# U-phase of an expert layer: the high and low parts of the tokens pass the high weights in one 512-column product

## The chip, the cores and the metric

The kernel runs on one core of a Trainium2 chip. The metric is the device time of one execution in microseconds, as a median of several runs. Beside it there is one profiled execution, with a trace of every engine: TensorE (PE, with its weight loads as PEld), VectorE (DVE), ScalarE (ACT), GpSimd (POOL) and SyncE (SP), which issues the loads of the weights.

## The reference, cut to what matters

Two transformer blocks run one after the other on 256 tokens of width 1024. The last part of the second is an expert layer with 16384 experts of one neuron each; it takes about half of the time. The change lies in it alone.

```python
def peer_ffn(h, w_query, sub_keys, expert_u, expert_v):
    q = jnp.einsum('bsd,dk->bsk', h, w_query).reshape(B, S, PEER_HEADS, 2, PEER_HALF)
    sc = jnp.einsum('bshpc,hpnc->bshpn', q, sub_keys, ...)
    s1, i1 = lax.top_k(sc[..., 0, :], PEER_TOPK)          # 16 of 128 keys
    s2, i2 = lax.top_k(sc[..., 1, :], PEER_TOPK)
    ...                                                   # 16 of the 16 x 16 sums
    gates = jax.nn.softmax(top_s, axis=-1)
    def chunk(args):
        u = expert_u[ec]
        a = jax.nn.gelu(jnp.einsum('cd,chkd->chk', xc, u), approximate=False) * wc
        return jnp.einsum('chk,chkd->cd', a, expert_v[ec])
```

## The kernel before

The kernel gathers nothing. It computes the activation of all 16384 experts for all 256 tokens, keeps gelu of it in a tile `G` of 128 x 128 x 256, multiplies `G` by a matrix of gates that is zero for experts not chosen, and multiplies the result by all of `expert_v`.

**Two-part products.** Every float32 operand is split in two parts that TensorE takes at full rate: `split` (L288) makes the high part H by a copy on ACT (L289) and the low part L as the source minus H on DVE (L290). A product is then three matmuls, H by L, H by H and L by H, added up in one PSUM bank (`mm3`, L315).

**The U-phase** (L1683 on) runs over 128 blocks of 128 experts. For block i, `wload` issues one DMA of 512 KB (`raw`), splits it into `wh` and `wl` (three buffers each), and `fm_mm` (L327) multiplies it by the tokens `h = (hH, hL)` in 8 steps of the contraction, with three matmuls of 256 columns each, 24 in all (L323, L324, L325). The bank that takes the result is one of four (`mm`, L1436). ScalarE reads it and applies gelu. For the tokens whose gates are in `G` already (the first `td`), gelu goes to a tile `ge`, and DVE multiplies it into `G` (L1638, L1639); for the others it goes straight to `G` (L1635).

**The background** shares the engines with the U-phase. It is a list `bg`, from which `run(UC)` takes some work after each block, by costs written in the code: first the selection on DVE (`half` and `cand` with their top-16 steps, `rowcol`, `lookup`), then `gates`, which transposes the chosen indices on PE into an `mm` bank of its own (L1584 to L1594), then 64 groups of four tokens (`wgroup`): one-hot matrices on DVE (`onehots`, L1605 to L1608, once for two groups), eight small matmuls on PE (L1619, L1620), and the result times `G`, on DVE for blocks that are done (L1625) and by a copy on ACT for the others (L1627).

**What sets the order.** Each engine works through its own instructions in order. That order is made when the program is built: a scheduler with a timeline of its own mixes the U-blocks and the background, by the order in the code and by what is ready in its timeline. It isn't decided on the chip.

After the U-phase comes the V-phase (L1705 on): 128 blocks with twelve matmuls of 512 columns each (L319 to L321).

Of the kernel before, what the change touches and what calls it, by code (L numbers as in the profile page):

```python
# [6 lines left out]
F32 = mybir.dt.float32  # L7
F32R = mybir.dt.float32r
# [4 lines left out]
AF = mybir.ActivationFunctionType  # L13
# [185 lines left out]
def _build(tc, nc, A, out, stop=99, dbg=None):  # L199
    ctx = ExitStack()  # L200
    mm_, act, dve, pool = nc.tensor.matmul, nc.scalar, nc.vector, nc.gpsimd
# [9 lines left out]
    hB = P("hB", side="right")  # L211
# [6 lines left out]
    hA = big.enter_context(TP("hA"))  # L218
# [27 lines left out]
    def mm_bank(shape=(128, 512)):  # L246
        return bank("mm", shape)
# [49 lines left out]
    def wload(ap, n=1024, p=None, g=None):  # L297
        return wsplit(wraw(ap, n), n, p, g)
# [28 lines left out]
    def fm_mm(ps, w, h, nk=8):  # L327

        for k in range(nk):
            mm3(ps, (w[0][:, k * 128:(k + 1) * 128], w[1][:, k * 128:(k + 1) * 128]),  # L330
                (h[0][:, k], h[1][:, k]), k == 0, k == nk - 1)

    def tm_mm(ps, h, k, c, w, n0, n1, start, stop):

        mm3(ps, (h[0][:, k, c * 128:(c + 1) * 128], h[1][:, k, c * 128:(c + 1) * 128]),
            (w[0][:, n0:n1], w[1][:, n0:n1]), start, stop, False)
# [93 lines left out]
    class Norm:  # L430
# [2 lines left out]


        def __init__(self, hp, gain, shift=None, on_dve=False):
            self.hH = hp.tile([128, 8, 256], F32R, tag="hH", name="hH")
            self.hL = hp.tile([128, 8, 256], F32R, tag="hL", name="hL")
            self.gain, self.shift, self.dve = gain, shift, on_dve
            self.kinds = ("mm",) * 4
            self.h = (self.hH, self.hL)  # L440
            self.s = {}
# [53 lines left out]
    class RawNorm:  # L495
# [3 lines left out]


        def __init__(self, hp, gain):
            self.hH = hp.tile([128, 8, 256], F32R, tag="hH", name="hH")
            self.hL = hp.tile([128, 8, 256], F32R, tag="hL", name="hL")
            self.gain, self.h = gain, (self.hH, self.hL)
            self.ss, self.y, self.v, self.half = {}, {}, {}, {}

# [209 lines left out]
    with TP("warm") as p:  # L716
        z = p.tile([128, 256], BF16, name="z")
        dve.memset(z, 0.0)
        ps = fill_bank((128, 256))
# [62 lines left out]
    def mixer(nin, nout):  # L782
        h = nin.h
# [17 lines left out]
        qrope = m.tile([128, 2, 256], F32, name="qrope")  # L801
        knope = m.tile([128, 4, 256], F32, name="knope")
        vm = m.tile([128, 2, 512], F32, name="vm")
        yH = hA.tile([128, 8, 256], F32R, tag="hH", name="yH")
        yL = hA.tile([128, 8, 256], F32R, tag="hL", name="yL")


        latent = {}
# [393 lines left out]
    def attention(nin, nout):  # L1202
        h = nin.h
# [38 lines left out]
        ps = mm_bank((16, 256))  # L1242
# [103 lines left out]
        pstack.close()  # L1346
        fctx.close()
        set_psum(acc=2, mm=2, sc=2, pt=2)
        yH = hA.tile([128, 8, 256], F32R, tag="hH", name="yH2")
        yL = hA.tile([128, 8, 256], F32R, tag="hL", name="yL2")  # L1350

        def y_tile(dt):

# [105 lines left out]
    def peer():  # L1459
# [168 lines left out]
            state["td"] = t0 + 4  # L1628

        def ublock(i):  # L1630
            ps = mm_bank((128, 256))
            fm_mm(ps, wload(A["pu"][i]), h)
            td = state["td"]
            if td < 256:
                act.activation(G[:, i, td:], ps[:, td:], AF.Gelu)  # L1635
            if td > 0:
                t = ps_.tile([128, 256], F32, tag="ge", name="ge")
                act.activation(t[:, 0:td], ps[:, 0:td], AF.Gelu)  # L1638
                dve.tensor_mul(G[:, i, 0:td], t[:, 0:td], G[:, i, 0:td])  # L1639
            state["cur"] = i + 1  # L1640

        from collections import deque
# [3 lines left out]
        def run(c):  # L1646
            nonlocal credit
            credit = min(credit + c, 4.0)
            while bg and credit > 0:
                cost, f = bg.popleft()  # L1650
                f()
                credit -= cost
# [3 lines left out]
        for i in range(17):  # L1656
            if i < 16:
                query(order[i])
            else:
                ublock(0)  # L1660
            if i == 0:
                continue
            nt = order[i - 1]
            scores()
            done.add(nt)
            for c in range(2):
                bg.append((1.1, lambda nt=nt, c=c: half(nt, c)))
            if nt ^ 1 in done:
                for c in range(2):
                    bg.append((1.4, lambda hd=nt // 2, c=c: cand(hd, c)))  # L1670
            run(QC)
# [9 lines left out]
            if g % 2 and late:  # L1681
                bg.append(late.popleft())
        for i in range(1, 128):  # L1683
            ublock(i)
            run(UC)
        while bg:
            bg.popleft()[1]()
        acc = [[acc_bank() for _ in range(2)] for _ in range(2)]
# [16 lines left out]
        for i in range(128 - VT):  # L1705
            if 8 <= i < 40 and i % 4 == 0:
                mod_step(32 + i // 4 + 6, g2p, g2)
            if i == 64:
                done = finish(G)
            if i == 96:  # L1710

                hs = [hB.tile([128, 2, 1024], F32R, tag=t, name="w" + t) for t in ("hH", "hL")]
                for k in range(2):
                    H, L = (h_[:, k] for h_ in hs)
                    split(wraw(A["pv"][126 + k]), H, L)
                    last.append((H, L))
            a = operands(G[:, i].rearrange("p (c n) -> p c n", c=2))
            w = wload(A["pv"][i], 1024, pv1 if i % 4 == 3 else None)
            for c in range(2):
                for j in range(2):  # L1720
                    out_mm(i, c, j, a[c], w)
# [91 lines left out]
```

## Time and profile before

| | |
|---|---|
| median of 3 runs | 1580.17 us (1578.63 to 1581.3) |
| profiled execution | 1577.72 us |
| its span, first to last instruction | 1575.6 us |
| granted TensorE clock, mean | 0.997 |
| PE busy | 1554.0 us, 99% |
| DVE busy | 1122.9 us, 71% |
| ACT busy | 812.9 us, 52% |
| POOL busy | 91.6 us, 6% |

The time of an execution is 2.1 us longer than the span. Busy shares are averages over the whole program; the stretches differ. In rows of the timeline, an instruction's duration reaches into the next one's, so the room that it takes on its engine is read from start to start.

### The profile page before, as it was taken

How to read it: one execution, taken by the hardware profiler on the slowest of the kernel's cores; microseconds unless marked ns; L12 is line 12 of the kernel's file. 1: busy time of each engine (PE TensorE's matmuls, PEld its weight loads, DVE VectorE, ACT ScalarE, POOL GpSimd, SP SyncE). 2: the span in 40 equal slices, each digit the busy share in tenths (PEclk: the TensorE clock that was granted, in tenths of full speed). 3: DMA queues.
4: the chain of work that ended last, by engine and by line, in shares of the span. 5: the costliest groups of instructions: out<-in, count | busy, mean ns of one | idle time of the engine just before them, and what ended most of it. 6: DMA issues, size and time to landing. Idle time of an engine off the chain costs nothing.

```text
span 1575.6 us, 27238 instructions
## 1 busy us (share of the span) xinstructions
PE 1554.0 (99%) x10352; PEld 1408.1 (89%) x10352; DVE 1122.9 (71%) x2210; ACT 812.9 (52%) x1557; POOL 91.6 (6%) x161
## 2 busy tenths in 40 slices
PE   9999999999999999999999999999999999999998
PEld 7999899879999879997899999999999887888886
DVE  7766768768856656556799989788996566555654
ACT  6444564555445676654554554544445445455543
POOL 1400011100000112011000000000000000000001
PEclk9999999999999999999999999999999999999999
DMA  8777754438976446441455655554456777666762
GB/s 310 251 253 245 254 168 137 141 104 306 336 218 226 157 155 201 134 135 54 179 166 182 185 182 167 161 157 157 156 161 190 256 228 235 193 189 189 221 187 91
DMA packets 84852, 299.94 MB, mean 190 GB/s; under 512 B 9616, under 2 KB 11248, under 8 KB 84336
## 3 DMA queue, kind: packets, MB, share of 16 engines
q1 hardware_dynamic: 81072, 290.92, 57.0%
q10 hardware_dynamic: 3648, 7.28, 1.3%
q8 instruction: 81, 1.33, 0.3%
q14 instruction: 51, 0.42, 0.1%
HBM read 294.95 MB, written 3.15 MB: 189 GB/s over the span
## 4 chain that ended last, share of the span: by engine, by line
PE 89%; DMA 5%; DVE 3%; ACT 2%; issue 1%; POOL 0%; SPq 0%; POOLq 0%; ACTq 0%; DVEq 0%
PE mm L323 15%; PE mm L324 15%; PE mm L325 15%; PE acc L319 12%; PE acc L321 11%; PE acc L320 11%; DMA raw<-in_pv 2%; DMA raw<-in_wmod 2%; ACT wh L289 1%; DVE wl L290 1%; PE acc L1619 1%; PE acc L1620 1%; PE acc L929 1%; PE sc L1271 1%; PE mm L1512 0%
## 5 line engine op out<-in xcount | busy, mean ns | idle before, releaser
L289 ACT ACTIVATE wh<-raw 128x1024 fp32r<-128x1024 f32 (+3 forms) x605 | 528.0, 897 | 539.2 <-PE mm L324 251.7
L290 DVE TENSOR_TENSOR wl<-raw,wh 128x1024 fp32r<-128x1024 f32 (+3 forms) x605 | 610.8, 1026 | 266.0 <-ACT wh L289 262.7
L323 PE MATMUL mm<-hL,wh 128*128 128x256 f32 x1976 | 565.0, 286 | 0.0
L325 PE MATMUL mm<-hH,wl 128*128 128x256 f32 x1976 | 560.0, 284 | 0.0
L324 PE MATMUL mm<-hH,wh 128*128 128x256 f32 x1976 | 559.6, 283 | 0.0
L323 PEld LDWEIGHTS mm<-hL,wh 128*128 128x128 f32 x1976 | 377.5, 191 | 2.8
L324 PEld LDWEIGHTS mm<-hH,wh 128*128 128x128 f32 x1976 | 377.6, 191 | 2.0
L325 PEld LDWEIGHTS mm<-hH,wl 128*128 128x128 f32 x1976 | 377.4, 191 | 0.4
L319 PE MATMUL acc<-wh,aL 128*128 128x512 f32 x648 | 256.1, 395 | 0.7 <-DVE aL L290 0.7
L321 PE MATMUL acc<-wl,aH 128*128 128x512 f32 x648 | 253.6, 393 | 0.0
L320 PE MATMUL acc<-wh,aH 128*128 128x512 f32 x648 | 253.3, 391 | 0.0
L321 PEld LDWEIGHTS acc<-wl,aH 128*128 128x128 f32 x648 | 121.7, 188 | 28.6 <-issue 0.2
L319 PEld LDWEIGHTS acc<-wh,aL 128*128 128x128 f32 x648 | 122.0, 188 | 27.1 <-DVE aL L290 2.5
L320 PEld LDWEIGHTS acc<-wh,aH 128*128 128x128 f32 x648 | 121.7, 188 | 26.7 <-issue 0.5
L319 PE MATMUL acc<-wh,hL 128*128 128x512 f32 x224 | 88.6, 397 | 4.1 <-DVE hL L520 2.3
L320 PE MATMUL acc<-wh,hH 128*128 128x512 f32 x224 | 87.3, 391 | 0.0
L321 PE MATMUL acc<-wl,hH 128*128 128x512 f32 (+1 forms) x224 | 85.2, 390 | 0.0
L290 DVE TENSOR_TENSOR aL<-G,aH 128x256 fp32r<-128x256 f32 x128 | 53.6, 419 | 3.4 <-ACT aH L289 3.4
L319 PEld LDWEIGHTS acc<-wh,hL 128*128 128x128 f32 x224 | 42.1, 188 | 13.5 <-ACT wh L289 2.4
L631 DVE SCALAR_TENSOR_TENSOR macc<-raw,col,macc 128x1024 f32<-128x1024 f32 x28 | 35.9, 1281 | 25.0 <-DMA raw<-in_wmod 24.8
L289 ACT ACTIVATE aH<-G 128x256 fp32r<-128x256 f32 x128 | 51.2, 401 | 4.0 <-PE acc L321 4.0
L594 ACT ACTIVATE sg<-sg 128x256 f32<-128x256 f32 x36 | 14.9, 413 | 69.8 <-DVE sg L593 66.5
(476 smaller groups left out, 1649.7 us busy)
## 6 DMA issues: line engine op xcount, KB each, us to landing
raw<-in_pu SPq DMA_DIRECT2D x128, 512.0 KB, 3.6
raw<-in_pv SPq DMA_DIRECT2D x128, 512.0 KB, 4.3
raw<-in_wmod SPq DMA_DIRECT2D x48, 512.0 KB, 4.9
raw<-in_w1gu SPq DMA_DIRECT2D x36, 512.0 KB, 4.4
raw<-in_w2gu SPq DMA_DIRECT2D x36, 512.0 KB, 4.7
raw<-in_w1d SPq DMA_DIRECT2D x22, 512.0 KB, 4.7
raw<-in_w2d SPq DMA_DIRECT2D x22, 512.0 KB, 4.5
raw<-in_wout SPq DMA_DIRECT2D x16, 512.0 KB, 3.6
```

The costliest lines, as they stand in the source:

```text
L289: act.activation(H, src, AF.Copy)
L290: lasts["low"] = dve.tensor_sub(L, src, H.bitcast(F32))
L319: mm_(ps, aL, bH, start=start, stop=False)
L320: mm_(ps, aH, bH, start=False, stop=False)
L321: lasts["pe"] = mm_(ps, aH, bL, start=False, stop=stop)
L323: mm_(ps, aH, bL, start=start, stop=False)
L324: mm_(ps, aH, bH, start=False, stop=False)
L325: mm_(ps, aL, bH, start=False, stop=stop)
L631: dve.scalar_tensor_tensor(macc[j], raw, K("c", k), macc[j], op0=OP.mult, op1=OP.add)
L929: mm_(ps[:, j, c], k[pr][:, j, sl], q[pr][:, j, sl], start=True, stop=True)
L1271: mm_(ps[:, o:o + n], qa[:, hd, c * 128:c * 128 + 128], ka[:, hd, 0:n], start=True, stop=False)
L1619: mm_(ps[:, j], H[:, j], O[:, j], start=True, stop=False)
```

## The change

The tokens' high and low parts now stand in one tile, `h`, side by side. In each of the 8 steps the high weights pass over both at once, in one matmul of 512 columns into a bank of two halves (high by high in the first, high weights by low tokens in the second). The low weights pass over the high tokens as before, into the first half. The two halves then have to be added: ACT copies the second half to the tile `ge` (now for every block), DVE adds the first half to it, and gelu reads the sum from `ge`. The multiplication of gelu with the gates goes from DVE to GpSimd. This second part, `upart`, stands behind `run(UC)` in the loop, where before the whole block stood ahead of it.

```diff
+    def fm_wide(ps, w, hw, nk=8):
+        for k in range(nk):
+            wH, wL = (w[i][:, k * 128:(k + 1) * 128] for i in range(2))
+            low = lambda: mm_(ps[:, 0], wL, hw[:, 0, k], start=False, stop=False)
+            if k == nk - 1:
+                low()
+            mm_(ps, wH, hw[:, :, k], start=k == 0, stop=k == nk - 1)
+            if k < nk - 1:
+                low()
...
-            self.hH = hp.tile([128, 8, 256], F32R, tag="hH", name="hH")
-            self.hL = hp.tile([128, 8, 256], F32R, tag="hL", name="hL")
+            self.both = hp.tile([128, 2, 8, 256], F32R, tag="h", name="h")
+            self.hH, self.hL = self.both[:, 0], self.both[:, 1]
...
         def ublock(i):
-            ps = mm_bank((128, 256))
-            fm_mm(ps, wload(A["pu"][i]), h)
+            ps = mm_bank((128, 2, 256))
+            fm_wide(ps, wload(A["pu"][i]), n6.both)
+            return ps
+
+        def upart(i, ps):
+            u = ps_.tile([128, 256], F32, tag="ge", name="ge")
+            act.activation(u, ps[:, 1], AF.Copy)
+            dve.tensor_add(u, ps[:, 0], u)
             td = state["td"]
             if td < 256:
-                act.activation(G[:, i, td:], ps[:, td:], AF.Gelu)
+                act.activation(G[:, i, td:], u[:, td:], AF.Gelu)
             if td > 0:
-                t = ps_.tile([128, 256], F32, tag="ge", name="ge")
-                act.activation(t[:, 0:td], ps[:, 0:td], AF.Gelu)
-                dve.tensor_mul(G[:, i, 0:td], t[:, 0:td], G[:, i, 0:td])
+                act.activation(u[:, 0:td], u[:, 0:td], AF.Gelu)
+                pool.tensor_mul(G[:, i, 0:td], u[:, 0:td], G[:, i, 0:td])
             state["cur"] = i + 1
...
-                ublock(0)
+                upart(0, ublock(0))
...
         for i in range(1, 128):
-            ublock(i)
+            ps = ublock(i)
             run(UC)
+            upart(i, ps)
```

The other tiles that share the old tags (`yH`, `yL` and a last pair of weights) are cut from a common tile in the same way. In the order below, L339 and L342 are the matmuls of `fm_wide` (low weights, high weights), L1651 is the new addition, and lines of the background stand 13 higher than before.

On PE, at the end of a U-block behind which a group of the background starts, the order before has three matmuls of 256 columns for each step:

```order
L323 MATMUL mm<-hL,wh 128x256
L324 MATMUL mm<-hH,wh 128x256
L325 MATMUL mm<-hH,wl 128x256
L1619 LDWEIGHTS B
L1619 MATMUL acc<-O,B 128x128
```

and the order now has two for each step, one of 512 and one of 256 columns:

```order
L342 MATMUL mm<-h,wh 128x512
L339 MATMUL mm<-h,wl 128x256 x2
L342 MATMUL mm<-h,wh 128x512
L1632 LDWEIGHTS B
L1632 MATMUL acc<-O,B 128x128
```

The 128 blocks lose 1024 matmuls and their weight loads; the groups of the background are as they were.

On DVE, at the place where the first groups of the background begin (B, BL and O are the one-hot tiles, L1570 to L1573 the lookups), the order before goes from one split of weights (`wl`) to the next after one to four other rows:

```order
L1570 TENSOR_TENSOR G_8535<-G_8535,iob_8551 128x2x256
L290 TENSOR_TENSOR wl_10978<-raw_10975,wh_10977 128x1024
L1607 TENSOR_TENSOR B_10911<-B_10911,slotT_8550 128x1024
L1583 TENSOR_TENSOR G_8535<-G_8535,gs_11970 128x128
L1572 TENSOR_TENSOR G_8535<-G_8535,idxf1_8545 128x2x256
L290 TENSOR_TENSOR wl_11016<-raw_11013,wh_11015 128x1024
L1605 TENSOR_TENSOR B_11048<-ioh_8553,slotT_8550 128x1024
L1608 TENSOR_TENSOR O_11047<-ioh_8553,slotT_8550 128x1024
L1573 TENSOR_REDUCE G_8535<-G_8535 128x32
L1606 TENSOR_TENSOR BL_11049<-B_11048,slotT_8550 128x1024
L290 TENSOR_TENSOR wl_11069<-raw_11066,wh_11068 128x1024
```

and the order now, at the same place, ends with the addition for the U-block whose bank is mm_10737 (L1618 to L1621 are the one-hot matrices, L1638 the product with `G`, L1583 and L1586 lookups):

```order
L1620 TENSOR_TENSOR B_10793<-B_10793,slotT_8542 128x1024
L290 TENSOR_TENSOR wl_10979<-raw_10976,wh_10978 128x1024
L1586 TENSOR_REDUCE G_8527<-G_8527 128x32
L1596 TENSOR_TENSOR G_8527<-G_8527,gs_11595 128x128
L1638 SCALAR_TENSOR_TENSOR G_8527<-acc_10680,G_8527 128x44x4
L1618 TENSOR_TENSOR B_10912<-ioh_8545,slotT_8542 128x1024
L1638 SCALAR_TENSOR_TENSOR G_8527<-acc_10720,G_8527 128x45x4
L1621 TENSOR_TENSOR O_10911<-ioh_8545,slotT_8542 128x1024
L1583 TENSOR_TENSOR G_8527<-G_8527,iob_8543 128x2x256
L1619 TENSOR_TENSOR BL_10913<-B_10912,slotT_8542 128x1024
L1651 TENSOR_TENSOR ge_10763<-mm_10737,ge_10763 128x256
```

The addition before this one, that for the bank mm_10697, stands 33 rows ahead; of the rows between, five are splits of weights, eleven one-hot matrices and seven lookups.

On DVE, late in the U-phase, the order before has the product with `G` of a U-block (L1639) between two splits:

```order
L290 TENSOR_TENSOR wl_13495<-raw_13492,wh_13494 128x1024
L1625 SCALAR_TENSOR_TENSOR G_8535<-acc_13381,G_8535 128x97x4
L1639 TENSOR_TENSOR G_8535<-ge_13371,G_8535 128x168
L1607 TENSOR_TENSOR B_13474<-B_13474,slotT_8550 128x1024
L290 TENSOR_TENSOR wl_13541<-raw_13538,wh_13540 128x1024
```

and the order now has the addition there, for two blocks of the same kind:

```order
L290 TENSOR_TENSOR wl_13531<-raw_13528,wh_13530 128x1024
L1618 TENSOR_TENSOR B_13551<-ioh_8545,slotT_8542 128x1024
L1621 TENSOR_TENSOR O_13550<-ioh_8545,slotT_8542 128x1024
L1651 TENSOR_TENSOR ge_13481<-mm_13440,ge_13481 128x256
L1619 TENSOR_TENSOR BL_13552<-B_13551,slotT_8542 128x1024
L290 TENSOR_TENSOR wl_13578<-raw_13575,wh_13577 128x1024
L1638 SCALAR_TENSOR_TENSOR G_8527<-acc_13470,G_8527 128x111x4
L1620 TENSOR_TENSOR B_13551<-B_13551,slotT_8542 128x1024
L1651 TENSOR_TENSOR ge_13521<-mm_13487,ge_13521 128x256
L1638 SCALAR_TENSOR_TENSOR G_8527<-acc_13510,G_8527 128x112x4
```

The product of gelu and gates is gone from DVE and stands alone on GpSimd, which had nothing to do in the U-phase.

## Rows read from the trace of the kernel before

**Rows 1.** The page: engine, busy us (share of the span) and instructions.

```profile
PE 1554.0 (99%) x10352; PEld 1408.1 (89%) x10352; DVE 1122.9 (71%) x2210; ACT 812.9 (52%) x1557; POOL 91.6 (6%) x161
```

**Rows 2.** Stretches of the U-phase: busy us (instructions) by engine, clock, DMA.

```profile
core 0: us, PE busy (x) PEld busy (x) DVE busy (x) ACT busy (x) POOL busy (x), PEclk, DMA share, GB/s
815.00:930.00 115.00, 115.00 (x960) 115.00 (x960) 104.30 (x371) 57.24 (x86) 0.00 (x0) 1.00 0.59 181
...
950.00:1060.00 110.00, 110.00 (x1023) 108.86 (x1022) 90.81 (x161) 55.61 (x131) 0.00 (x0) 1.00 0.53 162
1060.00:1190.00 130.00, 130.00 (x1220) 128.50 (x1219) 115.11 (x184) 60.17 (x154) 0.00 (x0) 1.00 0.50 158
```

**Rows 3.** The same view, ten microseconds before the first background group.

```profile
920.00:930.00 10.00, 10.00 (x85) 10.00 (x85) 5.48 (x11) 5.09 (x8) 0.00 (x0) 1.00 0.55 168
```

**Rows 4.** Timeline of PE, U-phase, first and last of 36: start us, us, instruction.

```profile
864.74 0.28 PE L323 MATMUL mm<-hL,wh 128*128 128x256 f32 x1
...
868.94 0.28 PE L325 MATMUL mm<-hH,wl 128*128 128x256 f32 x1
```

**Rows 5.** Timeline of PE, V-phase, first and last of 28.

```profile
1399.67 0.39 PE L320 MATMUL acc<-wh,aH 128*128 128x512 f32 x1
...
1405.87 0.39 PE L320 MATMUL acc<-wh,aH 128*128 128x512 f32 x1
```

**Rows 6.** Timeline of PE: one background group, and two matmuls behind it.

```profile
1051.86 0.23 PE L1619 MATMUL acc<-O,B 128*128 128x128 f16 x1
...
1052.29 0.36 PE L323 MATMUL mm<-hL,wh 128*128 128x256 f32 x1
1052.49 0.28 PE L324 MATMUL mm<-hH,wh 128*128 128x256 f32 x1
```

**Rows 7.** Groups by form, 800 to 1200 us: count | busy us, mean ns | idle before.

```profile
L290 DVE TENSOR_TENSOR wl<-raw,wh 128x1024 fp32r<-128x1024 f32 x127 | 155.1, 1221 | 46.2 <-ACT wh L289 45.5
L289 ACT ACTIVATE wh<-raw 128x1024 fp32r<-128x1024 f32 x127 | 134.5, 1059 | 191.1 <-PE mm L324 190.1 <-ACT G L1627 0.9
...
L1608 DVE TENSOR_TENSOR O<-ioh,slotT 128x1024 f16<-128x1024 f16 x32 | 21.8, 682 | 0.0
...
L1635 ACT ACTIVATE G<-mm 128x256 f32<-128x256 f32 x45 | 16.6, 369 | 0.0
L1570 DVE TENSOR_TENSOR G<-G,iob 128x512 bf16<-128x512 bf16 x16 | 10.9, 681 | 0.1
L1573 DVE TENSOR_REDUCE G<-G 128x32 f32<-128x512 bf16 x16 | 10.9, 681 | 1.0 <-PE mm L1586 0.8
...
L1572 DVE TENSOR_TENSOR G<-G,idxf 128x512 bf16<-128x512 bf16 x16 | 6.7, 420 | 0.1
```

**Rows 8.** Timeline of DVE: one block during the selection, from split to split.

```profile
840.89 1.20 DVE L290 TENSOR_TENSOR wl<-raw,wh 128x1024 fp32r<-128x1024 f32 x1
842.01 0.29 DVE L1522 MAX8 vals<-G 128x8 f32<-128x128 f32 x1
...
843.66 1.20 DVE L290 TENSOR_TENSOR wl<-raw,wh 128x1024 fp32r<-128x1024 f32 x1
```

**Rows 9.** Timeline of DVE, where GpSimd works beside it.

```profile
708.94 0.42 DVE L1325 TENSOR_TENSOR y<-mm,psc 128x256 f32<-128x256 f32 x1
709.28 0.68 DVE L290 TENSOR_TENSOR wl<-raw,wh 128x512 fp32r<-128x512 f32 x1
709.88 0.71 DVE L1318 TENSOR_TENSOR pd<-pf,pu 128x16 f32<-128x16 f32 x1
```

**Rows 10.** Timeline of POOL, the same two microseconds.

```profile
709.44 1.12 POOL L1326 TENSOR_TENSOR ga<-ga,y 128x256 f32<-128x256 f32 x1 [1.09 <-DVE y L1325]
```

**Rows 11.** The line of a GpSimd product: count, ns min/median/max, starts, forms.

```profile
L1326 POOL TENSOR_TENSOR ga<-ga,y x8: 732/745/1119, 610.7 to 719.9; 128x256 f32<-128x256 f32 x8
```

**Rows 12.** The same for the gelu product on DVE.

```profile
L1639 DVE TENSOR_TENSOR G<-ge,G x83: 156/285/421, 949.7 to 1214.3; 128x256 f32<-128x256 f32 x9, 128x8 f32<-128x8 f32 x2, 128x16 f32<-128x16 f32 x2, 128x24 f32<-128x24 f32 x2
```

**Rows 13.** The same for the product of group and G on DVE.

```profile
L1625 DVE SCALAR_TENSOR_TENSOR G<-acc,G x64: 334/502/646, 946.6 to 1187.9; 128x180 f32<-128x180 f32 x1, 128x184 f32<-128x184 f32 x1, 128x192 f32<-128x192 f32 x1, 128x196 f32<-128x196 f32 x1
```

More of the change, by code (lines that the diff above doesn't have):

```diff
@@ L501, in __init__ @@
         def __init__(self, hp, gain):
-            self.hH = hp.tile([128, 8, 256], F32R, tag="hH", name="hH")
-            self.hL = hp.tile([128, 8, 256], F32R, tag="hL", name="hL")
+            self.both = hp.tile([128, 2, 8, 256], F32R, tag="h", name="h")
+            self.hH, self.hL = self.both[:, 0], self.both[:, 1]
             self.gain, self.h = gain, (self.hH, self.hL)
@@ L803, in mixer @@
         vm = m.tile([128, 2, 512], F32, name="vm")
-        yH = hA.tile([128, 8, 256], F32R, tag="hH", name="yH")
-        yL = hA.tile([128, 8, 256], F32R, tag="hL", name="yL")
+        y_ = hA.tile([128, 2, 8, 256], F32R, tag="h", name="yH")
+        yH, yL = y_[:, 0], y_[:, 1]
         latent = {}
@@ L1348, in attention @@
         set_psum(acc=2, mm=2, sc=2, pt=2)
-        yH = hA.tile([128, 8, 256], F32R, tag="hH", name="yH2")
-        yL = hA.tile([128, 8, 256], F32R, tag="hL", name="yL2")
+        y_ = hA.tile([128, 2, 8, 256], F32R, tag="h", name="yH2")
+        yH, yL = y_[:, 0], y_[:, 1]
         def y_tile(dt):
@@ L1710, in peer @@
             if i == 96:
-                hs = [hB.tile([128, 2, 1024], F32R, tag=t, name="w" + t) for t in ("hH", "hL")]
+                hs_ = hB.tile([128, 2, 2, 1024], F32R, tag="h", name="wh_")
+                hs = [hs_[:, 0], hs_[:, 1]]
                 for k in range(2):
```

## The prediction

> **What bounds the kernel now.** I read the busy shares first, then the U-phase by stretches, then single blocks. The page has PE busy for 99% of the span and DVE for 71% [rows 1]; a gain has to come out of PE, unless another engine takes over. The stretches show where that can happen: in the U-phase PE has no idle time, and DVE is busy for 104.3 of 115 us during the selection, 90.8 of 110 when the background groups begin and 115.1 of 130 late [rows 2]. GpSimd does nothing there. The reader should see that DVE runs at 83 to 91% beside a full PE: a change that takes from PE and gives to DVE has little room. One hole stands out: DVE is busy for only 5.48 of the 10 us just before the first group begins [rows 3]. Selection was finished by then.
>
> The pace of PE is read from start to start: 35 steps from 864.74 to 868.94 us are 0.1200 us for a matmul of 256 columns [rows 4], so 24 of them make a block of 2.88 us. In the V-phase 27 steps take 6.20 us, 0.2296 us for 512 columns [rows 5]. The durations, 0.28 and 0.39, overlap and are not the pace.
>
> **The change part by part: PE.** Three matmuls of 256 columns took 0.3600 us in each of 8 steps. One of 512 and one of 256 take 0.2296 + 0.1200 = 0.3496, so a block goes from 2.880 to 2.797 us, and 128 blocks save 10.6 us. The trace has no place where the two widths alternate. The upper bound is that 256 more columns cost only their own streaming, 0.1067 us at the granted 2.4 GHz (the clock column is 1.00 [rows 2]): 0.2267 for the wide one, 0.0133 saved in a step, 13.6 us in all. The lower bound is nothing saved; a loss would need a wide matmul of over 0.24 us, and 27 in a row took 0.2296. I take 10.6, since the V-phase row has exactly the wide form. The weights of the group matmuls are untouched; a group puts 1052.49 - 1051.86 - 0.12 = 0.51 us between two U-matmuls [rows 6].
>
> The Trainium skill (TensorE: Matmul & The Clock Gate, Back-to-back issue gap) gives 262 cycles for 256 columns and 518 for 512, as an isolated gap. By it a step would save only 6 cycles, 2.5 ns, and the phase 2.6 us. Rows 4 and 5 show 120.0 and 229.6 ns in place of 109 and 216, so here a fixed part goes with each matmul, and that is what the change removes.
>
> **ACT.** A copy of 256 columns out of PSUM is new for each block, 0.37 us by the gelu row of that shape [rows 7]. With the split (1.06), the two gelus and a group's copy ACT needs about 2.2 us of a block of 2.8 or more. I cost it at nothing; it waited 190 us of the stretch for PE [rows 7]. Should that cover go, each block would show 0.37.
>
> **DVE.** An addition of 256 columns with one operand in PSUM takes 0.42 us, and the next instruction starts 0.34 after it [rows 9]; likewise 0.68 for a one-hot row means a room of about 0.60, and 1.22 for a split about 1.12 to 1.14 [rows 7, 8]. So every block gets 0.34 us more on DVE. What goes is the gelu product: 83 of them at a median of 0.285 [rows 12], with a room of about 0.2, and all of them late. The first 46 blocks lose nothing and gain 0.34.
>
> *Selection.* From 815 to 930 us there were 40 blocks with 104.3 us of DVE, 2.61 each [rows 2]. At the new pace 40 blocks last 111.9 us, and the same work with additions is 104.3 + 13.6 = 117.9. About 6 us of selection don't fit and must move behind. The order now shows this: each block there has one split, one addition and some 1.2 us of selection, together 2.66 us by the rooms above, still below 2.797. Nor is the addition late: the split behind it is for a block three further on, about 2 us before PE needs it. So I expect PE at its full new pace here, and the price later.
>
> *Where the groups begin.* There the lookups left over meet the first one-hot matrices. Between the additions for mm_10697 and mm_10737 DVE has five splits (5.7 us at 1.14), eleven one-hot rows (6.6 at 0.60), seven lookups (five at 0.60, two at 0.34: 3.7), two products with G (0.5) and seven small rows (1.3): 17.8 us. With 0.9 from the end of PE's block to the first addition (the copy's 0.37 and a row or two of DVE), some 1.3 of waits for the transposed indices and for a free split buffer, and 0.34 for the second addition it is 20.3. Meanwhile PE may do four blocks, one of them in the bank that the transposes give back (11.2), four groups (2.0) and the transposes (0.2), 13.4 us; then no bank is free until the second addition. PE stands still for about 6.9 us. I take 6.5. If DVE were ahead at that point, 3; if waits add up, 9.
>
> *Late blocks.* Two blocks now have on DVE two splits (2.28), two additions (0.68), four one-hot rows (2.40) and two products with G (late ones up to 0.646 [rows 13], so 1.0): 6.36, or 3.18 each. PE needs 2.797 + 0.95 x 0.51 = 3.28, with 0.95 groups per block counted in the order (before: 3.37). That fits, barely, if nothing else comes to DVE.
>
> **GpSimd.** The product with the gates takes GpSimd 0.73 to 0.75 us at 256 columns when alone [rows 11], less for fewer; it has the time. The question is what it does to DVE. At 709.44 us such a product starts while DVE splits weights; it lasts 1.12 us, 0.4 longer, and the DVE instruction behind the split, of 16 columns only, lasts 0.71 us and ends when GpSimd ends [rows 9, 10]. The two had excluded each other, and DVE lost about 0.55 us. So a product costs DVE between 0 and 0.55 us at full width, in proportion less at lower td. In the late order an addition or a product with G, which read PSUM, often stands behind the split; I assume that every other product hits: 0.1 to 0.25 us per block. DVE then needs about 3.35 against PE's 3.28 in the last 33 blocks with groups: 2.3 us, of which the lead of the splits takes a little. I take 2.0; the bounds are 0 (no collision) and 10 (all collide: 3.18 + 0.4 - 3.28 = 0.3, times 33).
>
> The Trainium skill (SBUF — State Buffer, Who interferes with whom) has this as a rule: a DVE instruction with two SBUF inputs contends with a GpSimd instruction that reads SBUF, and the second waits until the first is done. Rows 9 and 10 agree, 0.71 us for 16 columns. By that rule the new addition is safe, and the splits and one-hot rows are not; it is the case of the second rival.
>
> **Sum.** -10.6 + 6.5 + 2.0 = -2.1 us on a profiled execution of 1577.72 (span 1575.6 and 2.1 around it): 1575.6. The median of the runs is 2.45 higher than the profiled execution, so 1578.1.
>
> **Rivals.**
> *DVE keeps up.* If the built order is looser than my sum, with the transition at 2 us or less and no collisions, PE's saving stays: -8 to -13 us, about 1569. For it: PE never waited before, at 91% of DVE. Against: the hole of 4.5 us [rows 3] and more are spent.
> *GpSimd's products stop DVE.* From the point where td is over about 100 and DVE's room is under 0.1 us per block, every collision lengthens the U-phase. With all of them hitting in the late blocks (+10), 7 at the transition and the saving of 10.6, it is +6; with 2 or 3 us more among the middle blocks, +9: 1586 to 1589. For it: rows 9 and 10, and 4.68 of DVE's 6.36 us for two late blocks have both inputs in SBUF. Against: GpSimd waits too, and often for an instruction followed by one that reads PSUM.
> *The wide matmul saves nearly nothing.* If 256 and 512 columns cost in proportion when they alternate, 2.6 us are saved, the transition still costs 6.5, the late blocks have room for DVE again, and it is +4: 1584. Against it stand rows 4 and 5.
>
> **How the numbers follow.** A change below 0.2%, 3.2 us, can't be told from none. The forecast, -7 to +2 us, has 0.48, of which 0.18 lies below -3.2 and 0.30 within; its own range is 1573 to 1582. DVE keeps up: 0.22, faster. GpSimd stops DVE: 0.22, slower. The wide matmul saves nothing: 0.04, slower. The remaining 0.04 are other ways to no change. So faster 0.40, same 0.34, slower 0.26. Leaving out the lowest tenth (most of the saving kept) and the highest (over +9), the range is 1569 to 1588.
>
> **What the profile will show.** Wide and narrow matmuls in the U-phase should start 0.35 us apart in pairs, and PE should lose 0.08 us per block during the selection. At the first groups PE should have one or two gaps, about 6 us together, the larger ended by the addition on DVE. DVE should be over 95% busy from there to the last group, with splits or one-hot rows of up to 0.5 us more beside GpSimd's products, and these of more than 1 us. I am wrong if PE shows gaps during the selection (additions too late there), if it shows none at the first groups, or if the late blocks are slower than the 3.37 us of before.

## The result and the profile after

The changed kernel takes 1590.26 us in the median of 6 runs (1586.91 to 1593.73), beside 1580.74 us for the kernel before (6 runs of the same comparison). The ratio is 1.0061, with a 95% interval of 1.0044 to 1.0078: slower by 0.6%. The prediction was 1578.1 us and no change, so it was wrong, and the time lies above its range. The profiled execution took 1587.95 us, 10.2 more than that of before.

The page of the changed kernel, part 1 (compare [rows 1]): PE works 3 us less, DVE 35 us more, ACT 49 us more, GpSimd 80 us more.

```profile
PE 1551.0 (98%) x9328; PEld 1350.6 (85%) x9328; DVE 1157.6 (73%) x2255; ACT 861.9 (54%) x1685; POOL 171.2 (11%) x245
```

The stretches of the U-phase in the changed kernel (columns and stretches as in [rows 2], with 950 to 1060 cut in two):

```profile
815.00:930.00 115.00, 115.00 (x665) 100.53 (x664) 110.98 (x421) 70.95 (x128) 0.00 (x0) 1.00 0.52 182
...
950.00:970.00 20.00, 13.85 (x95) 11.65 (x94) 19.38 (x36) 10.32 (x18) 1.40 (x3) 0.95 0.40 143
970.00:1060.00 90.00, 90.00 (x625) 77.64 (x625) 85.23 (x140) 58.03 (x143) 25.82 (x30) 0.99 0.44 153
1060.00:1190.00 130.00, 130.00 (x925) 111.66 (x924) 126.50 (x187) 79.69 (x196) 36.95 (x40) 1.00 0.46 160
```

PE has no idle time in the selection and none in the late stretch, though DVE is now at 97% in both. All of PE's idle time, 6.15 us, lies where the groups begin (950 to 970). The timeline of PE there, with idle time and what ended it in brackets:

```profile
956.36 0.39 PE L342 MATMUL mm<-h,wh 128*128 128x512 f32 x1
956.93 0.47 PE L342 MATMUL mm<-h,wh 128*128 128x512 f32 x1 [0.18 <-DVE slotT L1606]
...
959.55 0.40 PE L342 MATMUL mm<-h,wh 128*128 128x512 f32 x1
962.11 0.23 PE L1632 MATMUL acc<-O,B 128*128 128x128 f16 x1 [2.17 <-DVE B L1620]
...
963.85 0.22 PE L1633 MATMUL acc<-O,BL 128*128 128x128 f16 x1
967.88 0.77 PE L342 MATMUL mm<-h,wh 128*128 128x512 f32 x1 [3.81 <-DVE ge L1651]
968.45 0.41 PE L339 MATMUL mm<-h,wl 128*128 128x256 f32 x1
968.67 0.63 PE L342 MATMUL mm<-h,wh 128*128 128x512 f32 x1
...
971.23 0.46 PE L342 MATMUL mm<-h,wh 128*128 128x512 f32 x1
```

First PE waits for the bank of the transposed indices, which DVE reads (`slotT`), and for a one-hot matrix, then, with all four banks full, for the addition (L1651). That addition and the one before it in DVE's order:

```profile
948.72 0.42 DVE L1651 TENSOR_TENSOR ge<-mm,ge 128x256 f32<-128x256 f32 x1
...
967.41 0.42 DVE L1651 TENSOR_TENSOR ge<-mm,ge 128x256 f32<-128x256 f32 x1
```

They start 18.7 us apart. After the wait for the addition the pairs of matmuls start 0.64 us apart. The windows of PE say why (us, busy, granted clock, DMA):

```profile
968.00:970.00 2.00, 2.00 (x7) 0.50 0.05 12
970.00:972.00 2.00, 2.00 (x10) 0.66 0.00 0
972.00:974.00 2.00, 2.00 (x19) 1.00 0.00 0
```

For 3.35 us the granted clock is at its lower level, 1.2 in place of 2.4 GHz. Five pairs take 3.35 us (967.88 to 971.23) instead of 1.76, so 1.6 us are lost on top of the 6.15. (Read from start to start, less the pace of the matmul ahead, the three waits took 0.34, 2.33 and 3.97 us, 6.6 in all: the idle times in brackets begin only at the end of a duration, which reaches into the next row.)

Away from there a pair takes 0.352 us. In the timeline of PE during the selection, eleven pairs lie between these two starts, 3.87 us:

```profile
889.71 0.40 PE L342 MATMUL mm<-h,wh 128*128 128x512 f32 x1
...
893.58 0.40 PE L342 MATMUL mm<-h,wh 128*128 128x512 f32 x1
```

That is 2.815 us for a block, against 2.880 [rows 4].

To set a U-phase against another I take the time from the last score matmul ahead of it to the first matmul of the V-phase. In the timeline of PE, before:

```profile
813.18 0.60 PE L1512 MATMUL mm<-G,qT 128*128 128x128 f32 x4
...
1211.98 0.39 PE L319 MATMUL acc<-wh,aL 128*128 128x512 f32 x1
```

and after:

```profile
820.61 0.61 PE L1525 MATMUL mm<-G,qT 128*128 128x128 f32 x4
...
1219.55 0.40 PE L319 MATMUL acc<-wh,aL 128*128 128x512 f32 x1
```

The reader should see that the U-phase did not become longer: 398.8 us before, 398.94 after. The traces lie 7.4 us apart already where it begins, and the V-phase (first to last of these matmuls) adds 2.7: 354.33 before, 357.02 after. Ahead of the U-phase the two kernels issue the same instructions in the same order on every engine. So the experiments had to tell these theories apart: the shared tile costs time in all stages (P, and T for the early ones), the wide product costs time that the first trace doesn't show (W, and K for the start), the place of things in DRAM sets when weights land (D), or the rest is chance in when they land (U, C).

### The profile page after: what moved, and what is told of

Its sections match the earlier page's. It is cut to its first block, busy times and chain, and to the rows that moved or that the text cites. A ratio compares the mean times of both kernels' runs of the same rounds, so it can differ in the third digit from the quotient of the medians.

```text
span 1585.8 us, 25510 instructions
## 1 busy us (share of the span) xinstructions
PE 1551.0 (98%) x9328; PEld 1350.6 (85%) x9328; DVE 1157.6 (73%) x2255; ACT 861.9 (54%) x1685; POOL 171.2 (11%) x245
## 4 chain that ended last, share of the span: by engine, by line
PE 75%; DMA 10%; DVE 8%; issue 3%; ACT 2%; POOL 1%; SPq 0%; POOLq 0%; DVEq 0%; ACTq 0%
PE mm L342 15%; PE acc L319 10%; PE acc L321 10%; PE acc L320 10%; PE mm L339 8%; DMA raw<-in_wmod 6%; PE mm L323 5%; PE mm L324 5%; PE mm L325 5%; DVE wl L290 4%; DMA raw<-in_pv 2%; ACT wh L289 1%; PE acc L1632 1%; PE acc L942 1%; PE acc L1633 1%
## 5 line engine op out<-in xcount | busy, mean ns | idle before, releaser
L342 PE MATMUL mm<-h,wh 128*128 128x512 f32 x1024 | 362.1, 401 | 4.0 <-DVE ge L1651 3.8
L323 PE MATMUL mm<-h,wh 128*128 128x256 f32 (+1 forms) x952 | 271.5, 285 | 0.0
L325 PE MATMUL mm<-h,wl 128*128 128x256 f32 (+1 forms) x952 | 270.3, 284 | 0.0
L324 PE MATMUL mm<-h,wh 128*128 128x256 f32 (+1 forms) x952 | 269.8, 283 | 0.0
L339 PE MATMUL mm<-h,wl 128*128 128x256 f32 x1024 | 268.3, 282 | 0.0
L342 PEld LDWEIGHTS mm<-h,wh 128*128 128x128 f32 x1024 | 186.9, 189 | 38.0 <-DVE ge L1651 4.0
L339 PEld LDWEIGHTS mm<-h,wl 128*128 128x128 f32 x1024 | 194.0, 190 | 9.9
L323 PEld LDWEIGHTS mm<-h,wh 128*128 128x128 f32 (+1 forms) x952 | 181.6, 191 | 2.8
L324 PEld LDWEIGHTS mm<-h,wh 128*128 128x128 f32 (+1 forms) x952 | 181.6, 191 | 2.0
L325 PEld LDWEIGHTS mm<-h,wl 128*128 128x128 f32 (+1 forms) x952 | 181.5, 191 | 0.5
L1657 POOL TENSOR_TENSOR G<-ge,G 128x256 f32<-128x256 f32 (+37 forms) x84 | 80.8, 967 | 377.1 <-ACT G L1640 340.4
L319 PE MATMUL acc<-wh,h 128*128 128x512 f32 x224 | 88.8, 398 | 3.0 <-DVE h L506 1.6
L320 PE MATMUL acc<-wh,h 128*128 128x512 f32 x224 | 87.3, 391 | 0.0
```

What stands on the lines that cost most here:

```text
L319: mm_(ps, aL, bH, start=start, stop=False)
L320: mm_(ps, aH, bH, start=False, stop=False)
L323: mm_(ps, aH, bL, start=start, stop=False)
L324: mm_(ps, aH, bH, start=False, stop=False)
L325: mm_(ps, aL, bH, start=False, stop=stop)
L339: low = lambda: mm_(ps[:, 0], wL, hw[:, 0, k], start=False, stop=False)
```

## The experiments

Times are medians beside the kernel before on the same chip; each ratio has its 95% interval. "Start" is the last score, "U" the U-phase as just defined, "V" the V-phase, each from the one trace of that run.

| run | ratio to before | start | U | V |
|---|---|---|---|---|
| e1_tile_only | 0.9999 (0.9989 to 1.0009) | 817.66 | 398.79 | 355.26 |
| e12_tile_only_again | 0.9988 (0.9977 to 1.0000) | 819.43 | 398.80 | 354.35 |
| e11_before_again | 0.9998 (0.9989 to 1.0008) | 812.83 | 398.80 | 357.97 |
| e17_before_other_dram | 0.9988 (0.9974 to 1.0002) | 817.75 | 398.80 | 355.30 |
| e2_no_addition | 1.0013 (1.0000 to 1.0025) | 817.82 | 390.62 | 355.31 |
| e5_no_addition_again | 0.9990 (0.9977 to 1.0004) | 816.76 | 390.63 | 355.55 |
| e13_no_addition_third | 0.9978 (0.9964 to 0.9992) | 819.04 | 390.64 | 356.01 |
| e14_no_addition_two_tiles_early | 0.9983 (0.9971 to 0.9994) | 825.64 | 390.63 | 356.64 |
| e9_wide_late_no_addition | 1.0005 (0.9990 to 1.0019) | 819.27 | 394.67 | 356.08 |
| e10_wide_early_no_addition | 1.0022 (1.0003 to 1.0040) | 827.33 | 394.81 | 355.74 |
| e3_narrow_first | 1.0051 (1.0037 to 1.0066) | 822.08 | 393.61 | 356.21 |
| e18_narrow_first_again | 0.9994 (0.9984 to 1.0005) | 817.13 | 393.61 | 355.81 |
| e16_narrow_first_two_tiles_early | 0.9995 (0.9982 to 1.0008) | 818.53 | 393.60 | 356.61 |
| e19_narrow_first_two_tiles_again | 1.0009 (0.9994 to 1.0024) | 822.71 | 393.61 | 357.50 |
| after | 1.0061 (1.0044 to 1.0078) | 820.61 | 398.94 | 357.02 |
| e6_after_again | 1.0051 (1.0033 to 1.0068) | 821.70 | 398.99 | 357.21 |
| e15_after_two_tiles_early | 1.0036 (1.0019 to 1.0052) | 817.14 | 398.99 | 358.86 |
| e20_after_other_dram | 1.0034 (1.0020 to 1.0049) | 820.08 | 399.89 | 357.25 |
| e4_routing_on_vector | 1.0112 (1.0092 to 1.0133) | 823.31 | 403.40 | 360.41 |

e1 to e4 shared one chip; so did e5, e6, e9 and e10; e11 to e13; e14 to e17; e18 and e19; e20 had its own.

**e1_tile_only, e12_tile_only_again.** The kernel before with the layout alone, in both classes of normalised tokens, the two `y` tiles and the last weights of the V-phase:

```diff
-            self.hH = hp.tile([128, 8, 256], F32R, tag="hH", name="hH")
-            self.hL = hp.tile([128, 8, 256], F32R, tag="hL", name="hL")
+            self.both = hp.tile([128, 2, 8, 256], F32R, tag="h", name="h")
+            self.hH, self.hL = self.both[:, 0], self.both[:, 1]
```

> The kernel before with only the layout changed: high and low part of the tokens in one tile, all products, additions and routing as before. Theory P (the layout costs): the two traces lie 7.4 us apart already where the U-phase starts (after the last score 820.61 against 813.18) and 2.6 us more behind it, though nothing but the tiles differs there, so this kernel is 7 to 10 us slower than before, about 1589. Theory U (the U-phase costs, the rest is chance in when weights land): 1580.7, within 2 us of before.

> The kernel before with the shared tile alone, for a second trace and time. Theory C: last score anywhere from 813 to 822, median within 0.1% of before. Theory K, if the tile were what moves the start: 817 to 818 again as in its first trace. U-phase 398.8 in either.

1579.68 and 1579.52 us, no difference from before. The shared tile costs nothing; theory P falls.

**e2_no_addition, e5_no_addition_again, e13_no_addition_third.** The changed kernel with

```diff
-            u = ps_.tile([128, 256], F32, tag="ge", name="ge")
-            act.activation(u, ps[:, 1], AF.Copy)
-            dve.tensor_add(u, ps[:, 0], u)
+            ps = ps[:, 0]
```

and from there gelu from `ps` and the product with the gates on DVE, as in before.

> After with the wide product, but GELU takes the half of the high tokens' product straight from PSUM and the routing is back on VectorE: it leaves out the sum with the half of the high weights and low tokens. No copy, no addition, no product on GpSimd. Without the addition TensorE does not stall at the first groups (7.8 us in after: 0.18 + 2.17 + 3.81 idle and about 1.65 of halved clock) and keeps 128 x 0.06 = 7.7 us. Theory P: 1590.3 - 7.8 = about 1582 to 1583. Theory U: 1580.7 - 7.7 = 1573.

> The same kernel as e2_no_addition (it leaves out the sum with the half of the high weights and low tokens), for a second trace. In its first trace the U-phase took 390.6 us against 398.8 before (8.2 saved, last score to first product of the V-phase), yet its median was 3.6 us above before's, at a granted clock of 0.994 to 0.996 in the runs of 1581 to 1584 us against 0.998 to 0.999 in those of 1575. Theory C (weights that land late, outside the U-phase, whatever the kernel): U-phase 390 to 391 again, the rest of the span anything between the lowest and highest seen; a median near 1573 to 1580 this time is as likely as 1583. Theory W (the wide product itself costs time that the first trace did not happen to show): again 1581 to 1584, and the trace shows stretches of halved clock or idle TensorE inside or behind the U-phase.

> The wide product without addition (it leaves out the sum with the half of the high weights and low tokens) a third time, beside the two above on one chip. U-phase 390.6 in either. Medians so far 3.6 us above before's and 1.8 below it, where the U-phase alone should give 8.2 below. Theory C: a median anywhere from 1572 to 1583, its mean over the three nearer to 1575 than to 1582. Theory K: again 5 to 10 us later than before outside the U-phase, so 1577 to 1583, last score 816 to 827.

In three traces the U-phase lasts 390.6 us, 8.2 less than before, and PE waits for nothing in it. The stretch where the changed kernel stood still, in e2_no_addition (columns as above):

```profile
950.00:970.00 20.00, 20.00 (x135) 17.23 (x135) 19.87 (x39) 11.08 (x25) 0.00 (x0) 1.00 0.49 166
```

DVE is as full as in the changed kernel, 19.87 of 20 us, but a bank no longer waits for DVE. So the stall comes from the addition, not from PE's pace. The medians, 1582.87, 1578.54 and 1577.12 us, do not show the 8.2 us: 3.6 more than before, then 1.8 and 2.6 less. The expectation of theory C, a mean nearer to 1575 than to 1582, failed: the mean of the three is 1579.5. Theory K's 1577 to 1583 and its start of 816 to 827 held in e13.

**e3_narrow_first, e18_narrow_first_again.** The first some 50 blocks are those of before:

```diff
+            if state["td"] < 16:
+                narrow(i)    # three products of 256 columns, gelu from PSUM
+                run(UC)
+                continue
             ps = ublock(i)
```

> After, but every block before the fifth group (some 50 blocks: the selection and the first groups) goes with the three narrow products of before and GELU straight from PSUM; the wide product, its addition and GpSimd's product only from there on. Takes the stall at the first groups away (7.8 us) and gives 50 x 0.06 = 3 us of the saving back. Theory P: 1590.3 - 7.8 + 3 = about 1585.5. Theory U: 1580.7 - 78 x 0.06 = about 1576. If the stall only moves to the first wide block: 1590 as after.

> The same as e3_narrow_first, beside e19 on one chip. Theory T (the shared tile in the early stages costs): 1586 to 1588 again and 6 to 8 us above e19. Theory C (chance in the start): within 3 us of e19, both 1577 to 1584. U-phase 393.6.

The U-phase is 393.6 us, 5.3 less than after, and PE shows no wait in it: the stall did not move to the first wide block. The time was 1587.24 us in the first run and 1579.32 in the second, on another chip, with the same U-phase. An interval from runs on one chip does not cover this.

**e4_routing_on_vector.**

```diff
-                pool.tensor_mul(G[:, i, 0:td], u[:, 0:td], G[:, i, 0:td])
+                dve.tensor_mul(G[:, i, 0:td], u[:, 0:td], G[:, i, 0:td])
```

> After with the routing product back on VectorE, GpSimd idle. If GpSimd's products hold VectorE up and that decides (the rival of the prediction), this is 3 to 8 us faster than after, 1582 to 1587. If not, VectorE has 0.27 us more in each late block, about 3.1 to 3.3 of TensorE's 3.33: 1590 as after, up to 1596 if it becomes the bound.

1596.41 us, 6 more than the changed kernel, the upper end of the second case. What PE waited for in the U-phase of this run (us, times, longest):

```profile
PE mm L342 <- DVE ge L1651: 5.3, 5, 3.8
PE acc L1632 <- DVE B L1620: 2.1, 1, 2.1
PE acc L1632 <- ACT G L1640: 0.8, 1, 0.8
PE mm L342 <- DVE slotT L1606: 0.2, 1, 0.2
```

The addition was late five times instead of once. GpSimd's products help: on DVE the same work costs more than the collisions do.

**e9_wide_late_no_addition, e10_wide_early_no_addition.** As e2_no_addition, with `if i < 64:` (e9) or `if i >= 64:` (e10) ahead of the narrow branch shown above.

> As e2_no_addition (no sum with the half of high weights and low tokens), but blocks 0 to 63 with the narrow products of before, which are complete; wide from block 64 on. Theory C: U-phase about 4 us shorter than before, the median 1575 to 1577. Theory W, if the cost comes from the late blocks: 1581 to 1583; if it comes from the selection: 1575.

> The mirror of it: blocks 0 to 63 wide, without the sum with the half of high weights and low tokens, blocks 64 to 127 narrow as before. Theory C: U-phase about 4 us shorter, the median 1575 to 1577. Theory W, if the cost comes from the selection stretch, where VectorE is busy 92% and TensorE now goes 2% faster: 1581 to 1583; if it comes from the late blocks: 1575.

Each half saves 4.0 to 4.1 us in the U-phase of its trace; the times are 1580.62 and 1584.64 us. Theory C had 1575 to 1577 for both: e9 misses all of its saving, e10 twice as much. Neither half alone holds the loss. e10's trace is one of a long execution (1588.95 us), and it puts the loss ahead of the U-phase: start at 827.33, while the U-phase is as short as it should be.

**e6_after_again, e11_before_again.** Both kernels unchanged, for a second trace.

> The changed kernel as it is, for a second trace and its time on another chip. U-phase 399 us again as in its first trace (398.9, against 398.8 before). Theory C: the rest of the span lies anywhere within the spread of before. Theory W: it is again some 7 to 12 us above before's first trace outside the U-phase, and the time is 1587 to 1592.

> The kernel before, unchanged, for a second trace. In the ten traces so far the U-phase repeats to 0.1 us per kernel (after 398.94 and 398.99, without addition 390.62 and 390.63), but its start, the last score, lies anywhere from 813.18 (before) to 827.33, with the same code ahead of it. Theory C (chance in when weights land, the first trace of before was an early one): last score at 816 to 822 this time, U-phase 398.8, and the time of that one execution accordingly 1580 to 1587. Theory K (the start depends on the kernel): 812 to 814 again, and 1577 to 1579.

1589.30 us against 1580.31 of before, and 1579.37 against 1579.74. The start of before came out at 812.83, as theory K had it. But its V-phase took 357.97 us: a wait of 1.8 us and a halved clock behind it, which its first trace did not have.

**e14 to e17, e19, e20.** e14, e15 and e16 (and e19, its repetition) give the stages in the pool hA their two tiles back, the `y` tiles among them; e17 and e20 enlarge the scratch tensor:

```diff
-            self.both = hp.tile([128, 2, 8, 256], F32R, tag="h", name="h")
+            if hp is hA:
+                self.hH = hp.tile([128, 8, 256], F32R, tag="hH", name="hH")
+                self.hL = hp.tile([128, 8, 256], F32R, tag="hL", name="hL")
+            else:
+                self.both = hp.tile([128, 2, 8, 256], F32R, tag="h", name="h")
...
-    spill = nc.dram_tensor("spill", (128, 2 * D), F32, kind="Internal").ap()
+    spill = nc.dram_tensor("spill", (128, 34 * D), F32, kind="Internal").ap()
```

> As e2_no_addition (it leaves out the sum with the half of the high weights and low tokens), but the stages that use the pool hA (the first one, up to 200 us, among them) have separate tiles for high and low part as in before. Theory T (the shared tile in the early stages delays the start): last score back at 812 to 815, U-phase 390.6, time 1571 to 1574. Theory C (the program ahead is the same, the delay is chance): last score 816 to 822 as in the others, time 1575 to 1582.

> The changed kernel with separate tiles in the pool hA as in before. Theory T: last score 812 to 815, time 1589.5 - 7 = about 1582. Theory C: 1587 to 1592 as after. U-phase 399 in either.

> As e3_narrow_first (narrow products and GELU straight from PSUM until the fifth group, wide with addition from there), with separate tiles in the pool hA. U-phase 393.6 as in e3_narrow_first, 5.2 less than before. Theory T: about 1577, faster than before by 0.2 to 0.3%. Theory C: 1583 to 1588.

> The kernel before, with the scratch tensor in DRAM 16 MB larger, so that what is laid out behind it lies elsewhere; no work and no order changed. If the place of the weights in DRAM sets when they land, last score off 813 by 3 us or more and the median off before's by 2 us or more, either way. If not: 1579 to 1580.5 and 812 to 814.

> The same as e16_narrow_first_two_tiles_early, beside e18 on one chip. Theory T: 1578 to 1580, at or below before. Theory C: anything from 1577 to 1588, within 3 us of e18. U-phase 393.6.

> The changed kernel with the scratch tensor in DRAM 16 MB larger, as e17 did with before; no work and no order changed. U-phase 399.0, as in all its traces. Theory D (where things lie in DRAM sets when early weights land, and so the start): last score away from 817 to 822, towards 813 or beyond 824, and the median off 1586 to 1590 by 3 us or more. Theory C (chance from one execution to the next, whatever the layout): last score 817 to 822, median 1586 to 1590.

With two tiles the start is at 825.64, 817.14, 818.53 and 822.71: theory T falls. Theory C did not have all of it either: e14's start lies outside its 816 to 822, e15's 1586.34 us just under its 1587, and e16's 1579.8 us between the 1577 of T and the 1583 to 1588 of C. On one chip e18 and e19 are 1 us apart (1579.32 and 1580.27). In e17 the start moved from 813 to 817.75 with no change of work. A first loss is at one place in all traces but those of before and e11, where PE waits some 2.5 us for activations that DVE makes late. PE and its clock, 185 to 205 us, in before, in e11_before_again and in e17_before_other_dram:

```profile
185.00:205.00 20.00, 20.00 (x105) 1.00 0.63 207
```

```profile
185.00:205.00 20.00, 20.00 (x104) 1.00 0.69 220
```

```profile
185.00:205.00 20.00, 17.45 (x77) 0.91 0.74 250
```

Yet e17's median, 1578.75 us, is not above before's 1580.49 (the expectation asked for a shift of 2 us, and it is 1.7). Its profiled execution took 1583.26 us, one of the longest of its twelve, as the profiled ones of e1 and e12 were. So the start in one trace is not the start of the median execution.

A second place stands just ahead of the scores, where PE waits for the load of the keys. What PE waited for, before, and after, there with the late activations beside it:

```profile
PE mm L1512 <- DMA G<-in_keys: 0.2, 1, 0.2
```

```profile
PE mm L1525 <- DMA G<-in_keys: 3.9, 1, 3.9
PE acc L319 <- DVE aL L290: 3.0, 2, 2.5
```

The load took 5.8 us from issue to landing before and 8.9 after. Over all 20 traces it took 8.5 to 8.9 us in six (after, e4, e10, e14, e19, e20), and 5.7 to 6.3 in the other nine with wide blocks and in the five with narrow ones; in the six PE waits 2.9 to 3.9 us and the granted clock is at its lower level behind it. In every trace the start, less PE's idle time ahead of it and half of the time at the lower clock, comes to 798 to 802 us. So the spread of the starts is made of such waits and of what they do to the clock; why the load takes longer in some executions was not tested.

For e20 theory C had the start and the time right, 820.08 and 1586.63 us; moving things in DRAM did not bring the time back. Its U-phase, 399.89, is 0.9 longer than expected: there the granted clock was at 0.50 from 963 to 973 us.

## Why the prediction was wrong

**PE: right in kind, too large.** I took 0.3496 us for a pair by adding two rows. It measured 0.352, so a block saves 0.065 us in place of 0.083. The U-phase without the addition is 8.2 us shorter, not 10.6. The saving shows that a part of a matmul's time does not go with its columns, 8 ns for each of the 1024 left out. The isolated gap of the Trainium skill (TensorE: Matmul & The Clock Gate, Back-to-back issue gap), cited in the prediction, would have given 2.6 us; here the measurement decides.

**Selection: right.** PE goes at its full new pace, DVE is at 111 of 115 us, and no addition is late there.

**The first groups: right in place, order and size, but not complete.** Predicted was a stall of 6.5 us in one or two gaps, the larger ended by the addition; there were 0.18, 2.17 and 3.81, together 6.16, and 6.6 from start to start. The backlog of DVE between the two additions was 18.7 us, where the prediction had 17.8 of rows and 1.3 of waits. Not priced was what the wait does to PE's clock: 1.6 us more, 8.2 in all. e3_narrow_first takes it away by not letting banks wait for DVE there.

**Late blocks: the collisions came, the cost did not.** The groups of DVE instructions in the late stretch (1070 to 1190 us; count, busy us, mean ns, idle before), changed kernel:

```profile
L290 DVE TENSOR_TENSOR wl<-raw,wh 128x1024 fp32r<-128x1024 f32 x36 | 45.0, 1250 | 1.0 <-ACT wh L289 1.0
L1618 DVE TENSOR_TENSOR B<-ioh,slotT 128x1024 f16<-128x1024 f16 x17 | 17.2, 1009 | 0.0
L1651 DVE TENSOR_TENSOR ge<-mm,ge 128x256 f32<-128x256 f32 x37 | 15.3, 415 | 2.0 <-ACT ge L1650 2.0
```

and e4_routing_on_vector, where GpSimd does nothing there:

```profile
L290 DVE TENSOR_TENSOR wl<-raw,wh 128x1024 fp32r<-128x1024 f32 x35 | 42.8, 1223 | 4.1 <-ACT wh L289 4.0
L1651 DVE TENSOR_TENSOR ge<-mm,ge 128x256 f32<-128x256 f32 x36 | 15.2, 421 | 0.3
...
L1618 DVE TENSOR_TENSOR B<-ioh,slotT 128x1024 f16<-128x1024 f16 x16 | 11.0, 686 | 0.0
```

Beside GpSimd's product the first one-hot row of each four takes 1009 ns in place of 686, the splits 27 ns more, and the addition, which reads PSUM, nothing more. One such hit in the timeline of GpSimd and of DVE:

```profile
1133.80 1.20 POOL L1657 TENSOR_TENSOR G<-ge,G 128x184 f32<-128x184 f32 x1 [0.32 <-ACT G L1640]
```

```profile
1134.48 1.07 DVE L1618 TENSOR_TENSOR B<-ioh,slotT 128x1024 f16<-128x1024 f16 x1
1135.48 0.68 DVE L1621 TENSOR_TENSOR O<-ioh,slotT 128x1024 f16<-128x1024 f16 x1
```

The one-hot row lies over the last 0.5 us of the product (which ends at 1135.00) and lasts 0.39 longer than the one behind it, as in [rows 9, 10]. The Trainium skill (SBUF — State Buffer, Who interferes with whom) has the two share one port pair under an exclusive lock; the trace agrees, with 686 and 1009 ns. By the means, two blocks lose 0.32 on the row and 0.05 on two splits, some 0.19 us per block: the size I had assumed. But DVE stayed just inside PE's time, 126.5 of 130 us, and PE never waited for it. The term of 2.0 us was about nothing: of 398.94 - 390.62 = 8.3 the waits at the first groups take 6.6 and the clock behind them 1.6, which leaves 0.1.

**The sum of the U-phase: nearly right, in part by luck.** Predicted -10.6 + 6.5 + 2.0 = -2.1; measured -8.2 + 8.2 + 0.1 = +0.1. The saving was 2.4 us too large and the clock was left out, but the late term that did not come made up for half of it. Of the rivals none happened: DVE did not keep up, and the wide matmul saves most of what it should. (Had the two widths cost in proportion to their columns, as that rival says, nothing would have been saved, not its 2.6 us.) The time, 1590.26 us, lies close to the 1586 to 1589 of the rival in which GpSimd stops DVE, but that is not its cause: PE never waited for DVE in the late blocks.

**The step that failed: the sum was taken for that of the whole program.** I put nothing on what lies outside the U-phase. The ratios of the four runs of the changed kernel and its close variants (after, e6, e15, e20) average 1.0046, about 7.2 us; the U-phase has 0.1 of them (1.1 in e20). The V-phase has 2.2: 357.6 us on average in these four traces, 355.4 in the five with the narrow products throughout. The waits there can be named. What PE waited for in the V-phase, before and after:

```profile
PE acc L319 <- DVE aL L290: 0.7, 1, 0.7
```

```profile
PE acc L319 <- DVE aL L290: 2.4, 5, 0.8
```

The mechanism behind these waits was not tested further. About 5 us must lie ahead of the U-phase or behind the V-phase. In the traces the start is 7.4 us later, and 3.7 of these are the wait for the keys and some 2.5 the wait for late activations, as shown above; how much of that the median execution has is not known. Some 6 us are missing wherever else blocks are wide: without the addition the four ratios average 0.9991, 1.4 us faster, where U and V together (-8.2 and +0.4) should give 7.8; narrow first the four average 1.0012, 1.9 us slower, where -5.2 and +1.1 should give 4.1 faster. With the shared tile alone nothing is missing.

That this goes with the wide blocks and is not chance can be read from the table: a run's median less its U-phase is 1180.0 to 1181.9 us in the five runs with narrow blocks throughout, and 1185.7 to 1193.6 in the fifteen with wide ones. Even the fastest executions show it: the traces of e2 and e5 are of executions of 1574.85 and 1574.0 us, 2.9 and 3.7 under the 1577.72 of before's, where the U-phase saves 8.2, with starts of 817.82 and 816.76 against 813.18. A part of it is the clock. The mean granted clock over all executions is 0.9959 to 0.9970 in the four runs without the addition and 0.9971 to 0.9978 in the runs of before beside them; by an estimate from these differences (0.0007 to 0.0012 of some 1575 us), the former lose 1.1 to 2.0 us more to it.

What is shown: the cost of adding the halves. On one chip e6 stands 10.8 us above e5, on another e15 stands 8.0 above e14, where the traces give 8.4 for the U-phase and 1.7 to 2.2 for the V-phase. What stays open is why the wide product's 8 us do not come out as time, when the instructions ahead of the U-phase are the same. One rival was not tested: programs with wide blocks hold fewer instructions (up to 1024 fewer matmuls), so that what stands behind them in the program lies elsewhere. The start, with the same instructions ahead of it, lies from 812.8 to 827.3 us over all traces; with wide blocks it averages 820.6, without 816.2, but the latter includes executions that were long for their kernel. Not tried was a kernel whose early stages never let PE wait, which would take this spread out of the comparison.

No version beats both kernels for certain. The narrow first blocks give back the whole loss of the change in three runs of four (0.9994, 0.9995, 1.0009), and end where the kernel before is.

## What to carry to other kernels

When one engine's in-order queue frees another's buffers, price the worst backlog of that queue against the number of buffers, then add what the wait does to TensorE's clock. A saving of half a per cent in one phase is to be read in that phase of the trace, over two or three traces; the time of the program can move by as much for other reasons, and an interval from one chip doesn't cover another. A sum for one phase is a forecast for the program only with a range for the others.

## What was not expected of the hardware

- A wait of 3.81 us was followed by 3.35 us at the lower clock, which cost 1.6 us more.
- The U-phase of one kernel repeats to 0.1 us from trace to trace and from chip to chip (one of the 19 traces in the table was 0.9 off), while the 800 us ahead of it, with the same instructions, differ by up to 14.5 us.
- One load of 1024 KB, issued at the same place of the program, took 5.7 to 6.3 us in 14 traces and 8.5 to 8.9 in six.
- The same kernel gave 1.0051 and 0.9994 against before on two chips, each with an interval of 0.10 to 0.15% to either side.
